# Seven products for two tiles also in the first output projection of a two-layer trunk

## The chip, the cores and the metric

One core of a Trainium2 chip runs the whole program. The metric is the device time of one execution in microseconds. A core has a matrix engine (TensorE, PE in the profile, with its weight loads as PEld), a vector engine (VectorE, DVE), a scalar engine (ScalarE, ACT), GpSimd (POOL) and SyncE (SP), which here only issues transfers. Each engine works through its own list of instructions in order; semaphores tie the lists together.

## The reference

The program computes one inference step of a trunk of two layers for 640 tokens (512 latent tokens and 128 context tokens), with 2048 features in float32:

```python
# for each layer l: 0 is "even", 1 is "odd"
shift, scale, gate = split(silu(cond) @ ada_w[l] + ada_b[l], 3)   # cond: c for latent, c_ctx for context tokens
h = rms_norm(x, norm_g[l]) * (1 + scale) + shift
p = h @ w_in[l]                      # 2048 -> q, k, v, gates, convolution inputs
y = mixers(p)                        # 2048 features: two mixers of 1024 each, each with a SiLU gate
x = x + gate * (y @ w_out[l])        # the output projection, 2048 -> 2048
```

The even layer's mixers are a banded attention and a short gated convolution; the odd layer's are a differential attention and a dense attention. Results are x after the second layer and the new keys and values of the context tokens. The projections have to be of float32 quality.

## The kernel before

*How a product is made.* Activations lie with the features on the 128 partitions: 16 tiles of 128 x 640, called k-tiles. A weight tile is 128 output columns, 16 k-tiles of 128 x 128. TensorE works in a shortened float32 format, so `split` (L242) writes each operand as a high part (ACT, L243) and a low part (DVE, L244), and `proj_q` (L268) adds three products: high x high, high x low, low x high. The tokens go in two halves of 320. A weight tile thus takes 16 x 3 x 2 = 96 matmuls of 128 x 128 by 320 columns.

*Single tiles.* `run_tiles` (L308) takes a list of weight tiles. The first three form a lead phase: for each quarter of four k-tiles the `make_h` function makes the activations (`y0_maker`, L1035, reads y back from DRAM and splits it), and the three tiles use them at once. Then come the other tiles, quarter by quarter; weights are loaded by SP some quarters ahead. After each quarter, `slot` (L300) lets waiting pieces of other work go on: the follow-up of a finished tile (`prep`), the attention (`attn`), and the "fill", a generator that does conditioning work with a rate per slot.

*Pairs.* `run_pairs` (L427) takes two weight tiles together as a 2 x 2 block product of Strassen's kind (Winograd's form): the 2048 features are cut in two halves of eight k-tiles, the tokens in two halves of 320, and seven products of 8 x 3 = 24 matmuls give what two single tiles make of 8. The products are Q1, Q2, N5, P6, P7, Q3, P4. On the weight side, sums of tiles are made on DVE (`operand`, L451, into the tiles sx and sf); on the activation side, four combinations of y (called forms T1 to T4) are made once, by `forms` (L1275). The products are put together by DVE in four pieces of scratch room, which are the memory of the rope tables (`tables`), no longer needed then. Only layer 1's output projection uses this: four single tiles, then six pairs (L1352 to L1395). It brings y in through buffers that are partly those of the odd layer's attention.

*Layer 0's output projection.* All 16 tiles are single (the call at L1102). `out_job` (L1059) adds gate times product to x0, which SP brings back from DRAM, keeps x1 in SBUF in 16 tiles of its own, has POOL save it to DRAM, and adds its squares into `acc` for the next norm. The last tile goes by token halves (`out_last`, L1074): while the second half multiplies, the norm factor of the first half is made. `h1_maker` (L1107) makes the normed input of layer 1 from the x1 tiles.

*Conditioning.* The 6144 columns of `ada_w` per layer go in blocks of 512. Some are made on TensorE at the start; sixteen are made on DVE beside other work: `ada_on_dve` (L171) loads 128 x 512 pieces and adds them up with two accumulations each (L184), 16 pieces a block, and then sums over partitions on TensorE (L190, L196). Nine blocks lie in input projection 0, four in output projection 0, and three, by halves of 256 columns, in input projection 1 (`ada_halves_on_dve`, L204).

*Order.* What follows what on an engine is written by the program in part, and in part set by the scheduler of the framework, which orders instructions by their dependencies. Memory comes from pools ("even", "mid", "odd", "fin"); a pool that opens over one that closed waits for the last users of the memory it lies on. The stretches are: input projection 0 to about 901 us, output projection 0 to 1148, input projection 1 to 2121, output projection 1 to 2347.

Of the kernel before, what the change touches and what calls it, by code (L numbers as in the profile page):

```python
# [11 lines left out]
F32 = mybir.dt.float32  # L12
# [34 lines left out]
N_FILL0 = 9  # L47
N_FILL1 = 13
FILL0 = 0.85
FILL1 = 1.2  # L50
FILL2 = 0.6
# [3 lines left out]
def trunk_kernel(ctx: ExitStack, tc: tile.TileContext, I: dict, O: dict):  # L55
# [115 lines left out]
    def ada_on_dve(blocks, tags=("acc0", "acc1", "adaw", "adaw", "adaw", "ada_sb2")):  # L171
        wt = tags[2:5]
        bufs = 3 if wt[0] == wt[1] else 1
        for l, cb in blocks:
            ap = pools["cur"]
            acc = [ap.tile([P, 512], F32, tag=tags[c], name=f"acc{c}", bufs=1) for c in range(2)]
            for kt in range(KT):
                w = ap.tile([P, 512], F32, tag=wt[kt % 3], name="adaw", bufs=bufs)
                nc.sync.dma_start(w, ada_src(l, cb, kt, 1).rearrange("p k n -> p (k n)"))
                for c in range(2):  # L180
                    if kt == 0:
                        V.tensor_scalar(acc[c], w, sT[:, kt, c:c + 1], None, ALU.mult)
                    else:
                        V.scalar_tensor_tensor(out=acc[c], in0=w, scalar=sT[:, kt, c:c + 1], in1=acc[c],  # L184
                                               op0=ALU.mult, op1=ALU.add)
                yield
# [5 lines left out]
            sb = ap.tile([P, 256], F32, tag=tags[5], name="ada_sb2", bufs=1)  # L192
# [10 lines left out]

    def ada_halves_on_dve(blocks):  # L204

        for l, cb in blocks:
            for h in range(2):
                ap = pools["cur"]
                acc = [ap.tile([P, 256], F32, tag=f"hacc{c}", name=f"hacc{c}", bufs=1) for c in range(2)]
                for kt in range(KT):  # L210
                    w = ap.tile([P, 256], F32, tag="hadaw", name="hadaw", bufs=3)
                    nc.sync.dma_start(w, I["ada_w"][l, kt * P:(kt + 1) * P, cb * 512 + h * 256:cb * 512 + (h + 1) * 256])
                    for c in range(2):
                        if kt == 0:
                            V.tensor_scalar(acc[c], w, sT[:, kt, c:c + 1], None, ALU.mult)
                        else:
                            V.scalar_tensor_tensor(out=acc[c], in0=w, scalar=sT[:, kt, c:c + 1], in1=acc[c],  # L217
                                                   op0=ALU.mult, op1=ALU.add)
                    yield
                s = psT()  # L220
                for c in range(2):
                    PE.matmul(s[32 * c:32 * c + 32, 0:256], ones, acc[c], start=True, stop=True,
                              tile_position=(0, 32 * c))
                sb = ap.tile([64, 256], F32, tag="hsb", name="hsb", bufs=1)
                A.copy(sb, s[0:64, 0:256])
                t = psT()
                for j in range(2):
                    PE.transpose(t[:, j * 64:(j + 1) * 64], sb[:, j * P:(j + 1) * P], ident[0:64, 0:64])
                add_bias(l, cb, t[:, 0:128].rearrange("p (j c x) -> p j c x", j=2, c=2)[:, :, :, 0], h, 2)
                ada_done(l, cb, h, 2)  # L230
                if h == 1:
                    ready.add((l, cb))
                yield
# [74 lines left out]
    def run_tiles(jobs, w_ap, make_h, fill=None, rate=0.0, ahead=None, order=(0, 1, 2, 3), before=None,  # L308
                  last=None, by_half=False, trans=[], grace=0, cut=None, summed=None, led=None):
# [84 lines left out]
        for i in range(lead, len(jobs)):  # L394
# [3 lines left out]
            for qd in range(4):  # L398
                proj_q(pp, parts[t], qd, qd, HV[:1] if split_last else HV)
                if before and qd == 0:  # L400
                    before(i)
                t += 1
                run_ahead(t)
                if pending and not prep:
                    n = pending.pop(0)
                    begin(jobs[n][1], pps[n])
                slot(fill, rate)
# [19 lines left out]
    def run_pairs(cols, w_ap, mov, room, begin, done, more):  # L427
# [46 lines left out]
        MOV = {"Q1": "B11", "Q2": "B21", "N5": "T1", "P6": "T2", "P7": "T3", "Q3": "B22", "P4": "T4"}  # L474
# [11 lines left out]
        def after(p, name, ps):  # L486
# [8 lines left out]
            elif name == "P6":  # L495
                V.tensor_sub(u2, ps, q1)
                V.tensor_sub(u4, st8["n5"], u2)
            elif name == "P7":
# [3 lines left out]
                more(p, u2)  # L502
            elif name == "Q3":
                V.tensor_add(u4, ps, u4)
                done(p, 0, 1, u4)
            else:
                done(p, 1, 0, ps)
# [4 lines left out]
        for i, (p, name) in enumerate(seq):  # L512
            ps, rows_ = pproj.tile([P, 512], F32, tag=f"p{'ab'[i % 2]}{i // 2 % 2}", name="pq")[:, 0:HALF], mov[MOV[name]]
            for h in range(2):
# [6 lines left out]
                if h == 0:  # L521
                    ahead(2 * i + 1)
            after(p, name, ps)
# [3 lines left out]
            elif name in ("P6", "P7"):  # L527
                load(p + 1, "A12" if name == "P6" else "A21")
                if name == "P7":
                    load(p + 1, "A22")  # L530
# [272 lines left out]
    fill1 = ada_on_dve(ada_rest[N_FILL0:N_FILL1])  # L803
    fill2 = ada_halves_on_dve(ada_rest[N_FILL1:])
# [227 lines left out]
    x1 = [None] * KT  # L1032
    make_y0 = y_maker(("q0h", "q0l", "q1h", "q1l"), NT)

    def y0_maker(k):  # L1035
        make_y0(k)
        if k == KT - 1:
            close("even")
            open_pool("mid")
            st["acc"] = pools["cur"].tile([P, NT], F32, name="acc")  # L1040

    def out_load(n):
        st["o", n] = pools["cur"].tile([P, NT], F32, tag="o", name="o", bufs=3)
        nc.sync.dma_start(st["o", n], x0dram[n // 4][:, n % 4 * NT:(n % 4 + 1) * NT])

    def out_before(n):
        if n == 0:
            out_load(0)
        if n + 1 < KT:
            out_load(n + 1)  # L1050

    def out_sum(n, pp, cs):
        if x1[n] is None:
            x1[n] = pools["cur"].tile([P, NT], F32, name=f"x1_{n}")
        for i, dsl, ssl, c in cs:
            V.scalar_tensor_tensor(out=x1[n][:, dsl], in0=pp[i][:, ssl], scalar=hgt[0][:, n, c:c + 1],
                                   in1=st["o", n][:, dsl], op0=ALU.mult, op1=ALU.add)

    def out_job(n):  # L1059
        def f(pp):  # L1060
            mp, acc = pools["cur"], st["acc"]
            need(0, n, fill0)
            out_sum(n, pp, CS)
            nc.gpsimd.dma_start(xdram[n], x1[n])
            if n == 0:
                A.activation(acc, x1[n], AF.Square)
            else:
                sq = mp.tile([P, NT], F32, tag="sq", name="sq", bufs=1)
                A.activation(sq, x1[n], AF.Square)
                V.tensor_add(acc, acc, sq)  # L1070
        return f


    def out_last(pp, h):  # L1074
        n, mp, sl = KT - 1, pools["cur"], HV[h][1]
        out_sum(n, pp, CS[:1] if h == 0 else CS[1:])
        if h == 0:
            st["sq"] = mp.tile([P, NT], F32, tag="sq", name="sq", bufs=1)
            st["rbc"] = mp.tile([P, NT], F32, name="rbc")
        A.activation(st["sq"][:, sl], x1[n][:, sl], AF.Square)  # L1080
# [15 lines left out]
        for b, (o, w) in enumerate(((0, P), (P, P), (2 * P, HALF - 2 * P))):  # L1096
            PE.matmul(rt[:, o:o + w], r[:, b:b + 1].to_broadcast([P, P]), ident[:, P - w:P], start=True, stop=True)
# [350 lines left out]
```

## Time and profile before

| | before |
|---|---|
| time, median of 3 runs | 2356.91 us (2353.24 to 2358.68) |
| profiled execution, time | 2356.86 us |
| profiled execution, span | 2354.9 us |
| TensorE busy | 2309.2 us (98%) |
| VectorE busy | 1477.3 us (63%) |
| ScalarE busy | 905.9 us (38%) |
| mean granted clock of TensorE | 0.995 |

The profile is that of one execution. Its page gives busy time of each engine, the span in slices, the transfers, the chain of work that ended last, and the costliest groups of instructions. In a group's line stand: line of the program and engine, operation, what is written from what (names without buffer numbers), the shape, how many; then busy time and mean ns of one; then the idle time of the engine just before them and what ended it. A row of the timeline gives start, duration, engine, line and operation, and in brackets the idle time before and what ended it. A row of the waits gives which instruction waited for which, the total, how often, and the longest. A row of the transfers gives how many, KB each and the median time from issue to landing. DMA "GB/s" is what all transfers of the core moved.

### The profile page before, as it was taken

The page shows a single profiled execution, that of the slowest core. Times are in us where ns is not written, and L with a number is a line of the kernel's source. Part 1 is how long each engine was busy: PE and PEld are TensorE (multiplying, and loading weights), DVE is VectorE, ACT ScalarE, POOL GpSimd, SP SyncE. Part 2 cuts the span into 40 slices and gives each one's busy share as a digit, 9 for nine tenths or more (in the row PEclk, how much of TensorE's full clock was granted, in tenths as well). Part 3 has the DMA queues.
Part 4 walks back from the last instruction along what each step waited for, and adds up shares of the span by engine and source line. Part 5 has one row for each costly group of instructions (what it writes and reads, how often), then busy time and mean ns, then how long its engine had stood idle before and what let it go on. Part 6 is the DMA issues. An engine that isn't in the chain of part 4 may idle for free.

```text
span 2354.9 us, 41103 instructions
## 1 busy us (share of the span) xinstructions
PE 2309.2 (98%) x16050; PEld 2229.7 (95%) x16050; DVE 1477.3 (63%) x2982; ACT 905.9 (38%) x1898; POOL 130.3 (6%) x175
## 2 busy tenths in 40 slices
PE   6999999999999999999999999999999999999998
PEld 3798999999999999999989999999999999999998
DVE  4459766756845565667874646556464754568775
ACT  4335432433422223222553443434434444445343
POOL 0001000000000000000010100001000001000001
PEclk9999999999999999999999999999999999999999
DMA  9984425425444445666442322313232212128542
GB/s 324 338 265 130 140 70 160 137 66 153 140 131 126 143 137 187 195 188 197 129 126 61 114 73 64 114 56 113 72 99 65 90 49 81 46 73 286 155 135 60
DMA packets 379729, 311.31 MB, mean 132 GB/s; under 512 B 17569, under 2 KB 323294, under 8 KB 379022
## 3 DMA queue, kind: packets, MB, share of 16 engines
q1 hardware_dynamic: 371968, 280.34, 39.4%
q0 software_dynamic: 7024, 28.12, 3.3%
q8 instruction: 126, 2.06, 0.4%
q14 instruction: 69, 0.57, 0.1%
q10 hardware_dynamic: 542, 0.22, 0.0%
HBM read 280.17 MB, written 28.44 MB: 131 GB/s over the span
## 4 chain that ended last, share of the span: by engine, by line
PE 79%; issue 12%; DVE 3%; DMA 2%; ACT 1%; POOL 1%; SPq 1%; ACTq 0%; POOLq 0%; DVEq 0%
PE pa L275 11%; PE pb L276 11%; PE pb L275 11%; PE pb L277 11%; PE pa L276 11%; PE pa L277 11%; PE T L692 2%; PE S L706 1%; PE S L705 1%; PE S L704 1%; PE T L158 1%; DMA ada<-in_ada_w 1%; PE T L753 1%; PE T L755 1%; PE T L754 1%
## 5 line engine op out<-in xcount | busy, mean ns | idle before, releaser
L243 ACT ACTIVATE wh<-raw 128x512 fp32r<-128x512 f32 (+1 forms) x514 | 321.1, 625 | 903.9 <-PE pb L276 762.9
L244 DVE TENSOR_TENSOR wl<-raw,wh 128x512 fp32r<-128x512 f32 (+1 forms) x514 | 350.8, 683 | 454.6 <-ACT wh L243 420.8
L275 PE MATMUL pa<-h,wh 128*128 128x320 f32 x1920 | 610.4, 318 | 1.5 <-ACT h L894 1.2
L276 PE MATMUL pa<-h,wh 128*128 128x320 f32 x1920 | 597.9, 312 | 0.6 <-DVE h L244 0.6
L277 PE MATMUL pa<-h,wl 128*128 128x320 f32 x1920 | 596.1, 310 | 0.0
L275 PE MATMUL pb<-h,wh 128*128 128x320 f32 x1920 | 595.1, 310 | 0.0
L277 PE MATMUL pb<-h,wl 128*128 128x320 f32 x1920 | 594.5, 310 | 0.0
L276 PE MATMUL pb<-h,wh 128*128 128x320 f32 x1920 | 594.3, 310 | 0.0
L275 PEld LDWEIGHTS pa<-h,wh 128*128 128x128 f32 x1920 | 361.9, 189 | 22.0 <-issue 16.9
L276 PEld LDWEIGHTS pa<-h,wh 128*128 128x128 f32 x1920 | 362.9, 189 | 5.0 <-issue 3.3
L277 PEld LDWEIGHTS pa<-h,wl 128*128 128x128 f32 x1920 | 362.3, 189 | 1.3 <-issue 1.2
L277 PEld LDWEIGHTS pb<-h,wl 128*128 128x128 f32 x1920 | 360.8, 188 | 2.5 <-issue 2.5
L276 PEld LDWEIGHTS pb<-h,wh 128*128 128x128 f32 x1920 | 360.9, 188 | 0.8 <-issue 0.8
L275 PEld LDWEIGHTS pb<-h,wh 128*128 128x128 f32 x1920 | 360.9, 188 | 0.6 <-ACT h L894 0.4
L184 DVE SCALAR_TENSOR_TENSOR acc<-adaw,sT,acc 128x512 f32<-128x512 f32 x390 | 275.5, 745 | 10.2 <-DMA adaw<-in_ada_w 9.8
L678 ACT ACTIVATE p<-S,nm,rq 128x768 f32<-128x768 f32 (+3 forms) x120 | 101.2, 844 | 112.9 <-DVE nm L673 84.6
L671 DVE TENSOR_REDUCE nm<-S 128x1 f32<-128x768 f32 (+3 forms) x120 | 91.9, 766 | 18.4 <-PE S L706 17.8
L243 ACT ACTIVATE pth<-T 128x512 fp32r<-128x512 f32 (+1 forms) x132 | 66.0, 533 | 68.1 <-PE T L692 65.9
L244 DVE TENSOR_TENSOR ptl<-T,pth 128x512 fp32r<-128x512 f32 (+1 forms) x132 | 77.7, 608 | 4.8 <-ACT pth L243 3.8
L217 DVE SCALAR_TENSOR_TENSOR hacc<-hadaw,sT,hacc 128x256 f32<-128x256 f32 x180 | 78.0, 478 | 3.1 <-DMA hadaw<-in_ada_w 2.9
L692 PE MATMUL T<-ident,p 128*128 128x128 f32 x452 | 65.1, 273 | 0.1
L520 PE MATMUL pq<-h,wl 128*128 128x320 f32 x192 | 60.1, 313 | 2.9 <-DVE wl L244 2.9
(300 smaller groups left out, 3015.9 us busy)
## 6 DMA issues: line engine op xcount, KB each, us to landing
adaw<-in_ada_w SPq DMA_DIRECT2D x208, 256.0 KB, 2.9
raw<-in_od_w_in SPq DMA_DIRECT2D x208, 256.0 KB, 2.8
raw<-in_ev_w_in SPq DMA_DIRECT2D x202, 256.0 KB, 2.9
ada<-in_ada_w SPq DMA_DIRECT2D x16, 2048.0 KB, 9.9
raw<-in_ev_w_out SPq DMA_DIRECT2D x64, 256.0 KB, 3.7
hadaw<-in_ada_w SPq DMA_DIRECT2D x96, 128.0 KB, 2.2
yd<-y POOLq DMA_DIRECT2D x34, 320.0 KB, 2.9
yin<-yd SPq DMA_DIRECT2D x32, 320.0 KB, 4.1
```

The source lines that it names most:

```text
L158: PE.matmul(acc[32 * g:32 * g + 32, 0:wd], sT[:, kt, :], w[:, kt % m, :], start=(kt < 4), stop=(kt >= KT - 4), tile_position=(0, 32 * g))
L184: V.scalar_tensor_tensor(out=acc[c], in0=w, scalar=sT[:, kt, c:c + 1], in1=acc[c], op0=ALU.mult, op1=ALU.add)
L217: V.scalar_tensor_tensor(out=acc[c], in0=w, scalar=sT[:, kt, c:c + 1], in1=acc[c], op0=ALU.mult, op1=ALU.add)
L243: A.activation(hi, x, AF.Copy)
L244: V.tensor_sub(lo, x, hi)
L275: PE.matmul(ps, wh[:, i, :], hi[:, sl], start=(j == js[0] if alone else (pos == 0 and j == 0)), stop=False)
L276: PE.matmul(ps, wh[:, i, :], lo[:, sl], start=False, stop=False)
L277: PE.matmul(ps, wl[:, i, :], hi[:, sl], start=False, stop=(j == js[1] - 1 if alone else (pos == 3 and j == 3)))
L520: PE.matmul(ps, wl[:, j, :], hi, start=False, stop=(h == 1 and j == 3))
L671: V.tensor_reduce(nm, s, axis=AX.X, op=ALU.max, negate=True)
L678: A.activation(p[:, 0:n], s, AF.Exp, scale=rsc, bias=nm, accum_out=l)
L692: PE.transpose(t[:, i * P:(i + 1) * P], p, ident)
```

## The change

`run_pairs`'s users become one function, `project_out(l, ...)`, that serves both layers, and layer 0's output projection now also goes as four single tiles and six pairs. What comes with it:

- The forms for layer 0 are made while its first tiles run. y comes through three `xr` buffers of 320 KB each, opened in the pool "mid" when the first y tile is made (before: four buffers of the even pool, and "mid" was opened after the last y tile). It is read twice, for the activations and for the forms.
- The x1 tiles are not kept: each is made in an `xr` buffer, saved to DRAM, its squares added, and given up. Six are read back during the last pair (`x1_tail`), eight at the first h of layer 1; the last two stay in their buffers. The rope tables, whose memory is scratch room now in layer 0 as well, are loaded again.
- The last two products of a pair change places (P4, then Q3), and `slot` is called after each half product as well. In the last pair the norm factors (`norm_half`) are made after P4 and after Q3.
- `h1_maker` writes the high part straight from ACT with the bias, and the low part with one DVE operation of the same input.
- The conditioning blocks: 12 in input projection 0 (before 9) at a rate of 1.2 (before 0.85); none in output projection 0; 4 in input projection 1 in parts of 256 columns, but with both parts in one accumulator and one pass over TensorE (before 3, by halves with two passes), at a rate of 0.9 (before 0.6) from the 25th quarter on.
- At the very end the rows of the last tile go out during Q3 and the last to go is the last but one.

```diff
-N_FILL0 = 9
-N_FILL1 = 13
-FILL0 = 0.85
-FILL1 = 1.2
-FILL2 = 0.6
+N_FILL0 = 12
+FILL0 = 1.2
+FILL1 = 0.9
+FILL1_FROM = 24
...
-        MOV = {"Q1": "B11", "Q2": "B21", "N5": "T1", "P6": "T2", "P7": "T3", "Q3": "B22", "P4": "T4"}
+        MOV = {"Q1": "B11", "Q2": "B21", "N5": "T1", "P6": "T2", "P7": "T3", "P4": "T4", "Q3": "B22"}
...
                 if h == 0:
                     ahead(2 * i + 1)
+                    slot()
             after(p, name, ps)
...
+    def late_yin(k):
+        t = pools["cur"].tile([P, NT], F32, tag="xr", name="yin", bufs=3)
+        nc.sync.dma_start(t, ydram[k])
+        split(*new_h(k), t)
...
     def y0_maker(k):
-        make_y0(k)
-        if k == KT - 1:
+        if k == 0:
             close("even")
             open_pool("mid")
             st["acc"] = pools["cur"].tile([P, NT], F32, name="acc")
+            st["sq"] = pools["cur"].tile([P, NT], F32, name="sq")
+            attn.append(forms())
+        late_yin(k)
...
+    def x1_done(n):
+        nc.gpsimd.dma_start(xdram[n], st["xr", n])
+        squares(n)
+
+    def x1_last(t, h):
+        n, sl = KT - 2 + t, HV[h][1]
+        if t == h:
+            squares(n, sl)
+            return
+        nc.gpsimd.dma_start(xdram[n], st["xr", n])
+        prep.append(norm_half(n, h))
+        if h:
+            drain(prep)
...
+    def x1_tail(name):
+
+        for k in (range(0, 4) if name == "P6" else range(4, 6)):
+            x1_back(k, big("w8", bufs=4) if k < 4 else big("sx" if k == 4 else "sf"))
+
+    def x1_back(k, t, i=0):
+        x1[k] = t[:, i * NT:(i + 1) * NT]
+        nc.sync.dma_start(x1[k], xdram[k])
+
+    project_out(0, y0_maker, x1_done, x1_last, x1_tail)
...
     def h1_maker(k, hv):
+        if k == 0 and hv[0][0] == 0:
+            for g in range(3):
+                t = big(f"T{g}")
+                for i in range(3 if g < 2 else 2):
+                    x1_back(6 + 3 * g + i, t, i)
+            for i in (14, 15):
+                x1[i] = st["xr", i]
+            nc.sync.dma_start(tables, I["k_tables"])
...
-            A.activation(t[:, sl], t[:, sl], AF.Identity, bias=mod[1][:, k, c:c + 1])
-        al = slice(hv[0][1].start, hv[-1][1].stop)
-        split(hi[:, al], lo[:, al], t[:, al])
+            A.activation(hi[:, sl], t[:, sl], AF.Identity, bias=mod[1][:, k, c:c + 1])
+        for sl, c in toks:
+            V.scalar_tensor_tensor(out=lo[:, sl], in0=t[:, sl], scalar=mod[1][:, k, c:c + 1], in1=hi[:, sl],
+                                   op0=ALU.add, op1=ALU.subtract)
```

The function that both layers now call:

```python
    def project_out(l, maker, finish, last, tail):
        w = W_OUT[l]
...
        go_on = run_tiles([(n * P, job(n)) for n in range(N_SINGLE - 1)], w, maker, order=(0, 2, 1, 3))
        n = N_SINGLE - 1
        parts = [split_w(load_raw(w, n * P, qd)) for qd in range(4)]
        go_on()
        pp = new_pp(0)
        for hv in (HV[1:], HV[:1]):
            for qd in range(4):
                proj_q(pp, parts[qd], qd, qd, hv)
                advance(attn, 2)
                go_on()
            if hv == HV[1:]:
                drain(attn)
                for j in range(8):
                    hi, lo = hs[j]
                    split(hi[:, HALF:NT], lo[:, HALF:NT], t1[j])
...
        run_pairs([(n * P, (n + 1) * P) for n in range(N_SINGLE, KT, 2)], w,
                  {"B11": half_of(0, 0), "T1": half_of(0, 1), "B21": half_of(8, 0), "B22": half_of(8, 1),
                   "T2": form_of(0), "T3": form_of(1), "T4": form_of(2)}, room, begin, part, done, tail)
        drain(prep)
```

361 lines of the change are left out of this document (161 added, 200 removed).

## The prediction

> **What bounds the kernel now.** I read the page's first part and the chain of waits, then the durations of the matmuls one by one, then busy time by stretch.
>
> ```profile
> span 2354.9 us, 41103 instructions
> PE 2309.2 (98%) x16050; PEld 2229.7 (95%) x16050; DVE 1477.3 (63%) x2982; ACT 905.9 (38%) x1898; POOL 130.3 (6%) x175
> PE 79%; issue 12%; DVE 3%; DMA 2%; ACT 1%; POOL 1%; SPq 1%; ACTq 0%; POOLq 0%; DVEq 0%
> ```
>
> TensorE is busy nearly all the time and carries the chain, so time goes with the matmuls and with TensorE's gaps. What one matmul costs is read from the timeline by their starts, since neighbours overlap:
>
> ```profile
> 1146.22 0.31 PE L275 MATMUL pb<-h,wh 128*128 128x320 f32 x1
> ...
> 1147.83 0.31 PE L277 MATMUL pb<-h,wl 128*128 128x320 f32 x1
> ```
>
> Each lasts 0.31, but eleven steps lie between these two starts: 1.61/11 = 146.4 ns each. Where DVE could come to bound is seen in busy time by stretch (columns: span, then busy time and instructions of PE, PEld, DVE, ACT, POOL, then granted clock, DMA share, GB/s):
>
> ```profile
> 160.00:400.00 240.00, 236.49 (x1680) 229.32 (x1679) 177.44 (x374) 99.27 (x226) 13.65 (x14) 1.00 0.47 142
> 400.00:600.00 200.00, 199.87 (x1416) 194.61 (x1415) 125.39 (x251) 79.35 (x176) 9.71 (x10) 1.00 0.38 112
> 2121.00:2187.00 66.00, 63.52 (x434) 62.56 (x434) 55.24 (x98) 34.65 (x58) 5.48 (x9) 1.00 0.93 296
> 2187.00:2200.00 13.00, 9.79 (x56) 9.25 (x55) 6.22 (x9) 2.86 (x6) 0.41 (x1) 0.87 0.38 101
> 2200.00:2340.00 140.00, 140.00 (x970) 139.91 (x969) 105.30 (x174) 57.25 (x103) 13.77 (x22) 1.00 0.40 113
> ```
>
> The last three rows are layer 1's output projection, which already works with four single tiles and six pairs. They are the nearest picture of what layer 0 becomes: the lead phase (all of y loaded, split and combined into forms) loses 2.5 us of TensorE, the start of the pairs loses about 3 in a gap, and the steady pairs lose nothing with DVE 75% busy. The waits of TensorE name the same places:
>
> ```profile
> PE T L543 <- DVE m L588: 5.5, 4, 3.1
> PE pq L520 <- DVE wl L244: 2.9, 1, 2.9
> PE T L543 <- ACT ot L1318: 2.3, 1, 2.3
> ```
>
> **The change part by part.**
>
> *Matmuls.* A tile takes 16 k-tiles x 3 products x 2 halves = 96 matmuls; a pair takes 7 x 24 = 168 where two tiles take 192. Six pairs save 6 x 24 = 144 matmuls: 144 x 146.4 ns = **-21.1 us**, all on the path. Both ends are the same here.
>
> *Conditioning passes on TensorE.* Each block ends with sums over partitions on TensorE:
>
> ```profile
> 901.05 0.31 PE L277 MATMUL pb<-h,wl 128*128 128x320 f32 x1
> 901.29 0.64 PE L190 MATMUL T<-acc,ones 128*32 128x256 f32 x8
> 901.86 0.41 PE L275 MATMUL pa<-h,wh 128*128 128x320 f32 x1
> ```
>
> From the matmul before to the one after are 0.81 us, 0.66 over the usual step, and two transposes follow: about 0.8 a pass, an estimate. Before there are 13 whole blocks and 3 in two halves, 19 passes; after, 16. Three passes fewer: **-2.4** (-3 to 0).
>
> *The boundary from input to output projection 0.* The rows above also show that there is no gap now: the first four y tiles were brought in earlier, into buffers that the old maker names. After, the maker closes the memory of the input projection when it makes its first tile, and loads y through three buffers that lie in that memory. Reading after's order of instructions: the first load on SP waits for the last gate multiplication of y, which waits for the last matmul of the input projection, and TensorE has no matmul in between that doesn't need this y. The chain of that tile, all of it now bare:
>
> ```profile
> 901.25 0.63 ACT L243 ACTIVATE wh<-raw 128x512 fp32r<-128x512 f32 x1 [2.89 <-PE pb L276]
> L967 ACT ACTIVATE gt_t<-pb 128x320 f32<-128x320 f32 x1 | 0.4, 418 | 0.0
> L968 DVE SCALAR_TENSOR_TENSOR gg<-gt_t,pb 128x320 f32<-128x320 f32 x1 | 0.5, 480 | 0.0
> L970 DVE TENSOR_TENSOR y<-y,gg 128x640 f32<-128x640 f32 x1 | 0.8, 818 | 0.0
> yin<-yd SPq DMA_DIRECT2D x32, 320.0 KB, 4.1
> adaw<-in_ada_w SPq DMA_DIRECT2D x208, 256.0 KB, 2.9
> L243 ACT ACTIVATE h<-yin 128x640 fp32r<-128x640 f32 x16 | 11.5, 732 | 12.0 <-DMA yin<-yd 8.2 <-PE pb L277 2.2 <-PE pb L276 1.5
> L244 DVE TENSOR_TENSOR h<-yin,h 128x640 fp32r<-128x640 f32 x16 | 13.0, 822 | 9.1 <-ACT h L243 9.0
> ```
>
> ACT splits a weight first (0.63), then tanh 0.42, DVE 0.48 and 0.82, the load 4.1, ACT 0.73: 7.2 us from the last matmul to the first. The first weights are ahead of it on SP; the next two y loads queue behind it and land together. After a gap the clock is slow for a while, as layer 1's start of the pairs shows:
>
> ```profile
> 2187.81 0.31 PE L519 MATMUL pq<-h,wh 128*128 128x320 f32 x1
> 2191.02 0.42 PE L520 MATMUL pq<-h,wl 128*128 128x320 f32 x1 [2.90 <-DVE wl L244]
> 2193.37 0.47 PE L518 MATMUL pq<-h,wh 128*128 128x320 f32 x1
> 2193.64 0.47 PE L519 MATMUL pq<-h,wh 128*128 128x320 f32 x1
> ```
>
> The step there is 0.27 instead of 0.146. The row of 2187 to 2200 has a mean clock of 0.87, so 13 x 0.13/0.5 = 3.4 us at half clock, which cost 3.4 x (1 - 0.146/0.27) = 1.5. With 0.7 for the second and third y tile, which need their DVE half (0.82) too: **+9.4**. Low end 6 (load at 2.9 and no slow stretch); high end 14 (an estimate: the load at 6.5 because the forms' loads share the engines, and a slow stretch of twice the length).
>
> *Lead phase.* Loads of y twice (2 x 16 x 320 KB) and four tiles of weights, eight sets of forms on DVE. Layer 1 does the same work and loses 2.5 us in the row of 2121 to 2187, most of it in one wait of 2.3 on an output copy that layer 0 doesn't have; but layer 1 has four further buffers for y and here there are three, and a y load that waits for one holds back the weight loads behind it on SP. I take **+2** (0 to 10; the high end is priced as a rival).
>
> *Start of the pairs.* Layer 1's stall (2.9 and the slow stretch, 5 in all) came from weight buffers that the forms held. In layer 0 the order of instructions puts the forms' end and the weight loads of the first pair well before the fourth tile ends, so I take **0** (0 to +5). Layer 1 keeps its own.
>
> *Steady pairs.* DVE gets saves to DRAM and squares with an addition per tile: 2 x 0.82 more in a pair's 168 x 0.146 = 24.6 us, on 105.3/140 = 75%: 82%. Nothing waits for it; **0** (0 to +3). POOL issues the saves; it is 6% busy.
>
> *Boundary to input projection 1.* Now:
>
> ```profile
> 1141.24 0.80 PE L1088 MATMUL T<-ones,sq 128*128 128x1 f32 x6 [0.46 <-DVE ss L1090]
> ...
> 1149.66 0.41 PE L276 MATMUL pa<-h,wh 128*128 128x320 f32 x1 [0.41 <-DVE h L244]
> 1152.07 1.54 PE L1097 MATMUL T<-ident,r 128*128 128x128 f32 x6 [0.70 <-POOL r L1093]
> 1155.52 0.47 PE L275 MATMUL pa<-h,wh 128*128 128x320 f32 x1
> ...
> 1158.61 0.33 PE L277 MATMUL pa<-h,wl 128*128 128x320 f32 x1
> ```
>
> Between 1147.83 and 1158.61 some 10.8 us pass for 24 matmuls of 146 ns (3.5): 7.3 lost, part of it to the norm of the last half, part to the slow clock. The norm of half 0 inside the last tile adds, with 0.8 for such a group of small matmuls and three groups, about 2: 9.3. After, the norm of half 0 runs under the last product (3.5 us of matmuls) and half 1's before the first matmul of layer 1: a chain as long as today's from 1147.83 to the first full-speed step, about 10 us from the last-but-one product to the first h, less 3.5 hidden, and 1.5 to 2 of slow clock: 8.3. **-1** (-3 to +5). The first x1 tiles are back by then; eight more (320 KB each) and the tables, 768 KB, are issued on SP after the last-but-one product and must land behind the first input matmuls.
>
> *Fills.* Input projection 0 takes three blocks more, 3 x 16 x 2 accumulations at 745 ns (the row of the accumulation):
>
> ```profile
> L184 DVE SCALAR_TENSOR_TENSOR acc<-adaw,sT,acc 128x512 f32<-128x512 f32 x390 | 275.5, 745 | 10.2 <-DMA adaw<-in_ada_w 9.8
> L217 DVE SCALAR_TENSOR_TENSOR hacc<-hadaw,sT,hacc 128x256 f32<-128x256 f32 x180 | 78.0, 478 | 3.1 <-DMA hadaw<-in_ada_w 2.9
> ```
>
> That is 96 x 0.745 = 71.5 us of DVE. The rate goes from 0.85 to 1.2 blocks' steps a slot, so the end of the filling stays about where it is; up to 600 us DVE goes from (177.4 + 125.4)/440 = 69% to some 84%, and in the first stretch from 74% to near 90%. In that stretch TensorE lost 240 - 236.5 = 3.5 us with 74%. **+3** (0 to +15). Input projection 1 gets 64 more steps of 256 wide, 64 x 0.478 = 31 us on a DVE that has room (its busiest waits, 5.5 us on the row of m, stay): **0** (-2 to +3).
>
> *Tail.*
>
> ```profile
> 2348.20 1.06 PE L543 MATMUL T<-ident,xr 128*128 128x128 f32 x5
> 2350.97 0.54 POOL L1321 DMA_DIRECT2D out_y_prompt<-ot  x1
> ```
>
> The last tile but one went out by POOL last, at 2351. After, one of the two last tiles goes out during the last product and the end hangs on the other half tile's short path through SP and ACT: **-1.2** (-2.5 to 0).
>
> Sum: -21.1 - 2.4 + 9.4 + 2 - 1 + 3 - 1.2 = -11.3. The profiled run took 2356.86 us (2.0 outside the span), the median of the runs is 2356.91, so both bases agree: **2345.5 us**.
>
> One rule of the Trainium skill comes out otherwise at the boundary to layer 1. "TensorE: Matmul & The Clock Gate", section "What's actually happening", says that the slow clock follows a whole idle window of about 3.4 us. By it the short waits there (0.4, 0.7 and the like) would cost no slow stretch after the change, and the sum would be 2343.5; this case's trace shows 0.27 steps at 1155.5 without one idle stretch of that length, so I keep the measured price.
>
> **The rivals.**
>
> *A. The first boundary is cheap.* The load of y may start before the gate is done if its buffer falls on memory freed earlier. Then 9.4 becomes about 1 and the rest stays: 2337. For it: today there is no gap at that place. Against: the first load's wait stands in after's instructions.
>
> *B. DVE becomes the bound in input projection 0, and it ends slower.* DVE works in order, so an accumulation ahead of a softmax step delays TensorE. At 74% the stretch to 400 us lost 3.5 us; at 90% a queue of 1.49-us pairs stands ahead of every urgent step. If four tenths of the 71.5 us come through as waits, +28.6 replaces +3: 2371. From a fifth (14.3) on, the gain is nil; for it speaks the wait of 3.1 on DVE's m, against it that 400 to 600 us lost 0.13 with 63%.
>
> *C. Loads bind the lead phase.* Three buffers, each held for a load and its two splits: at 4.1 + 0.73 + 0.82 = 5.65 us, 16 loads take 16 x 5.65/3 = 30 us, inside the 42 us that three tiles (288 matmuls) take; with loads at 6.5 under a DMA share of 0.93 they take 43 us and bind. Then lead +8 instead of +2, start of the pairs +4: 2355.5, no change.
>
> *D. x1 or the tables come back late.* Eight tiles and the tables, 3.3 MB at the 296 GB/s of the lead row: 11 us, beside weights; half of that bare gives about +5: 2350.5. For it: all of them are issued at the same moment as the first weights. Against: an h tile is wanted only every few us.
>
> *E. The saving doesn't appear.* If half products left gaps, the 144 would buy nothing; layer 1's 970 instructions in 140.00 busy us exclude that.
>
> **How the numbers follow.** My forecast's case (2337 to 2352, D included) gets 0.50, A 0.13, C 0.19, B 0.18. A measurement of this kernel tells 0.2% (4.7 us) from no change, so faster means below 2352.2: the forecast's case (0.50), A (0.13) and a little of C (0.04): 0.67. Same: most of C and a little of B: 0.15. Slower: most of B and C's worst: 0.18. The range goes from 2334 (A with a cheap boundary to layer 1) to 2364 (B half way); the likeliest case's own is 2337 to 2352.
>
> **What would show it.** Right: 144 fewer matmuls at 146 ns; one gap of about 7 us before the first matmul of the output projection, ended by ACT's h after a DMA yin, with steps of 0.27 behind it; steady pairs with TensorE 100% busy; TensorE waits in 160 to 600 us up by a few us only. Wrong: no gap there (A); PE waits on DVE in input projection 0 over 14 us (B); repeated waits for yin, or a gap at the first product of a pair in layer 0 (C); waits on x1 or tables after 1140 us (D).

## The result and the profile after

The changed kernel takes 2345.45 us (median of 5 runs, 2341.5 to 2347.92) where the kernel before takes 2354.12 us (median of 5, 2353.11 to 2358.68): a ratio of 0.9955, with a 95% interval of 0.994 to 0.9971. The profiled execution took 2347.92 us with a span of 2345.9, against 2356.86 and 2354.9 before: -9.0 us of span. The medians lie 8.7 us apart; the ratio stands for 10.6 us (6.8 to 14.1). The prediction said 2345.5 us, and -11.3 us on the profiled execution of before.

The first lines of the page of the changed kernel and its chain that ended last:

```profile
span 2345.9 us, 41233 instructions
PE 2286.9 (97%) x15900; PEld 2207.9 (94%) x15900; DVE 1577.8 (67%) x3187; ACT 932.9 (40%) x1934; POOL 129.7 (6%) x175
PE 87%; DMA 5%; DVE 4%; issue 2%; ACT 2%; SPq 1%; POOL 0%; ACTq 0%; DVEq 0%; POOLq 0%
```

TensorE is busy for 22 us less (2286.9 against 2309.2), but the span is only 9 us shorter: TensorE stands idle for 13 us more. A slow step counts as busy in this view. The waits of TensorE in the changed kernel name the largest one, which stands in no row of before:

```profile
PE pa L247 <- ACT h L215: 7.9, 2, 7.5
PE T L523 <- DVE m L568: 6.0, 4, 3.2
...
PE pa L248 <- DVE h L216: 2.8, 4, 1.1
```

Where it lies is seen best by stage. The projections' matmuls have a fixed number in each stage, so the start of the first and of the last of them marks the stage in every trace (in us; the columns add up to the span):

| stage | before | after | change |
|---|---|---|---|
| to the first projection matmul | 48.78 | 49.80 | +1.0 |
| input projection 0 | 867.34 | 871.19 | +3.9 |
| its last to output projection 0's first matmul | 0.15 | 7.77 | +7.6 |
| output projection 0, first 384 matmuls (four tiles) | 56.32 | 62.04 | +5.7 |
| output projection 0, the rest | 175.25 | 149.20 | -26.1 |
| boundary and the first 300 matmuls of input projection 1 | 51.94 | 51.28 | -0.7 |
| input projection 1, the rest | 926.87 | 927.55 | +0.7 |
| output projection 1 | 220.22 | 222.02 | +1.8 |
| last matmul's start to the end | 7.99 | 5.01 | -3.0 |

Each column is one execution, and single executions vary: three traces of the changed kernel have 870.5 to 871.7 in the second row, 61.7 to 66.4 in the fourth and 49.8 to 52.4 in the sixth. A change of 1 or 2 us in one row says little.

The timeline of TensorE in the changed kernel at the third row of the table:

```profile
920.99 0.31 PE L249 MATMUL pb<-h,wl 128*128 128x320 f32 x1
928.76 0.63 PE L247 MATMUL pa<-h,wh 128*128 128x320 f32 x1 [7.46 <-ACT h L215]
...
931.67 0.47 PE L249 MATMUL pa<-h,wl 128*128 128x320 f32 x1
931.94 0.47 PE L247 MATMUL pa<-h,wh 128*128 128x320 f32 x1
...
933.50 0.31 PE L248 MATMUL pb<-h,wh 128*128 128x320 f32 x1
933.64 0.31 PE L249 MATMUL pb<-h,wl 128*128 128x320 f32 x1
```

and the other engines in that gap:

```profile
921.19 0.63 ACT L215 ACTIVATE wh<-raw 128x512 fp32r<-128x512 f32 x1 [1.18 <-PE pb L248]
921.72 0.42 ACT L946 ACTIVATE gt_t<-pb 128x320 f32<-128x320 f32 x1
...
922.46 0.48 DVE L947 SCALAR_TENSOR_TENSOR gg<-gt_t,pb 128x320 f32<-128x320 f32 x1
922.97 0.82 DVE L949 TENSOR_TENSOR y<-y,gg 128x640 f32<-128x640 f32 x1
923.87 1.29 SPq L1064 DMA_DIRECT2D yin<-yd  x3
```

It is the chain that was forecast: tanh, the two DVE steps of the last gate, and only then the first load of y, which is split on ACT at 927.97. Behind the gap the steps are 0.27 us until 933.3, then 0.146. The granted clock goes with it (columns: window, its length, busy time and instructions of PE, PEld, DVE, ACT, POOL, granted clock, DMA share, GB/s):

```profile
920.00:926.60 6.60, 1.30 (x9) 1.03 (x8) 2.40 (x4) 0.96 (x3) 0.54 (x1) 1.00 0.51 134
926.60:933.40 6.80, 4.42 (x14) 3.72 (x15) 3.79 (x7) 2.80 (x4) 0.00 (x0) 0.50 0.99 371
```

It falls to half within the gap, at 926.6, and comes back at 933.4.

The windows of the changed kernel show the two stages that the forecast kept at nothing or nearly so (columns as above):

```profile
160.00:400.00 240.00, 236.11 (x1682) 228.61 (x1680) 194.54 (x407) 99.02 (x226) 13.33 (x15) 1.00 0.52 157
990.00:1139.00 149.00, 149.00 (x1020) 148.80 (x1019) 122.35 (x205) 63.69 (x104) 6.47 (x12) 1.00 0.47 140
```

With DVE at 81% instead of 74% in the first, TensorE is as busy as before (236.11 of 240 against 236.49). In the second, the steady pairs of layer 0, it is busy all the time with DVE at 82%.

At the boundary to layer 1 the steps are slow again, and at the end POOL is done with its last output while the matmuls still run:

```profile
1140.15 0.83 PE L1186 MATMUL T<-ident,r 128*128 128x128 f32 x6
1140.81 0.78 PE L1177 MATMUL T<-ones,acc 128*128 128x1 f32 x6
1141.94 0.80 PE L1177 MATMUL T<-ones,sq 128*128 128x1 f32 x6 [0.34 <-ACT sq L1169]
1144.18 0.88 PE L1186 MATMUL T<-ident,r 128*128 128x128 f32 x6 [1.45 <-POOL r L1182]
1144.88 0.73 PE L247 MATMUL pa<-h,wh 128*128 128x320 f32 x2
...
1145.67 0.47 PE L248 MATMUL pa<-h,wh 128*128 128x320 f32 x1
1145.93 0.47 PE L249 MATMUL pa<-h,wl 128*128 128x320 f32 x1
```

```profile
2340.70 0.76 POOL L1383 DMA_DIRECT2D out_y_sample<-ot  x1 [21.45 <-ACT ot L1382]
2340.84 0.31 PE L496 MATMUL pq<-h,wl 128*128 128x320 f32 x1
2341.45 0.54 POOL L1384 DMA_DIRECT2D out_y_prompt<-ot  x1
2342.71 0.39 SPq L1403 DMA_DIRECT2D out_y_sample<-ot  x1
2343.04 0.38 ACTq L1407 DMA_DIRECT2D out_y_prompt<-ot  x1
```

### The profile page after: what moved, and what is told of

Read it like the earlier page. It is cut to its first block, busy times and chain, and to the rows that moved or that the text cites. A ratio compares the mean times of both kernels' runs of the same rounds, so it can differ in the third digit from the quotient of the medians.

```text
span 2345.9 us, 41233 instructions
## 1 busy us (share of the span) xinstructions
PE 2286.9 (97%) x15900; PEld 2207.9 (94%) x15900; DVE 1577.8 (67%) x3187; ACT 932.9 (40%) x1934; POOL 129.7 (6%) x175
## 4 chain that ended last, share of the span: by engine, by line
PE 87%; DMA 5%; DVE 4%; issue 2%; ACT 2%; SPq 1%; POOL 0%; ACTq 0%; DVEq 0%; POOLq 0%
PE pa L247 10%; PE pb L247 10%; PE pb L248 10%; PE pb L249 10%; PE pa L248 10%; PE pa L249 10%; PE pq L494 4%; PE pq L496 4%; PE pq L495 4%; PE T L672 2%; DMA yin<-yd 2%; PE S L684 1%; PE S L686 1%; PE S L685 1%; DMA ada<-in_ada_w 1%
## 5 line engine op out<-in xcount | busy, mean ns | idle before, releaser
L247 PE MATMUL pa<-h,wh 128*128 128x320 f32 x1728 | 552.0, 320 | 10.6 <-ACT h L215 7.9
L248 PE MATMUL pa<-h,wh 128*128 128x320 f32 x1728 | 538.5, 312 | 2.8 <-DVE h L216 2.8
L249 PE MATMUL pa<-h,wl 128*128 128x320 f32 x1728 | 536.3, 310 | 0.0
L247 PE MATMUL pb<-h,wh 128*128 128x320 f32 x1728 | 535.8, 310 | 0.0
L249 PE MATMUL pb<-h,wl 128*128 128x320 f32 x1728 | 535.7, 310 | 0.0
L248 PE MATMUL pb<-h,wh 128*128 128x320 f32 x1728 | 535.1, 310 | 0.0
L187 DVE SCALAR_TENSOR_TENSOR acc<-adaw,sT,acc 128x512 f32<-128x512 f32 (+1 forms) x600 | 358.2, 640 | 16.3 <-DMA adaw<-in_ada_w 15.6
L247 PEld LDWEIGHTS pa<-h,wh 128*128 128x128 f32 x1728 | 326.5, 189 | 30.1 <-issue 14.9
L248 PEld LDWEIGHTS pa<-h,wh 128*128 128x128 f32 x1728 | 327.2, 189 | 8.5 <-issue 4.2
L247 PEld LDWEIGHTS pb<-h,wh 128*128 128x128 f32 x1728 | 325.3, 188 | 0.9 <-issue 0.4
L248 PEld LDWEIGHTS pb<-h,wh 128*128 128x128 f32 x1728 | 325.1, 188 | 0.1
L496 PE MATMUL pq<-h,wl 128*128 128x320 f32 x384 | 119.2, 311 | 3.1 <-DVE wl L216 3.1
L494 PE MATMUL pq<-h,wh 128*128 128x320 f32 x384 | 120.5, 314 | 0.3 <-DVE xr L1059 0.3
L495 PE MATMUL pq<-h,wh 128*128 128x320 f32 x384 | 119.1, 310 | 0.0
L495 PE MATMUL pq<-T,wh 128*128 128x320 f32 x288 | 88.8, 308 | 0.0
## 6 DMA issues: line engine op xcount, KB each, us to landing
ada<-in_ada_w SPq DMA_DIRECT2D x16, 2048.0 KB, 10.1
```

Source lines behind the costliest of these rows:

```text
L187: V.scalar_tensor_tensor(out=a, in0=w, scalar=sT[:, kt, c:c + 1], in1=a, op0=ALU.mult, op1=ALU.add)
L247: PE.matmul(ps, wh[:, i, :], hi[:, sl], start=(j == js[0] if alone else (pos == 0 and j == 0)), stop=False)
L248: PE.matmul(ps, wh[:, i, :], lo[:, sl], start=False, stop=False)
L249: PE.matmul(ps, wl[:, i, :], hi[:, sl], start=False, stop=(j == js[1] - 1 if alone else (pos == 3 and j == 3)))
L494: PE.matmul(ps, wh[:, j, :], hi, start=(h == 0 and j == 0), stop=False)
L495: PE.matmul(ps, wh[:, j, :], lo, start=False, stop=False)
```

## The experiments

My theory: the pairs give what their count of matmuls says, the late y loads at the first boundary take most of it back, and DVE is nowhere the bound. The rivals to be told apart: the DMA's share or DVE makes the loss wherever y is loaded; the fuller DVE in input projection 0 costs more than it seems; the moved conditioning blocks and not the pairs make the gain.

The stages of all traces (us, as in the table above; "boundary 1" is the third row, "four tiles" the fourth, "rest of out 0" the fifth):

| | after, again | early_y | fill16 | before_fill | both | warm | both_wide | after, third |
|---|---|---|---|---|---|---|---|---|
| to the first projection matmul | 49.28 | 49.12 | 50.20 | 51.17 | 49.27 | 50.79 | 48.83 | 50.66 |
| input projection 0 | 871.66 | 869.01 | 877.30 | 871.52 | 875.64 | 868.87 | 876.92 | 870.52 |
| boundary 1 | 7.19 | 0.15 | 7.52 | 0.15 | 0.15 | 9.01 | 0.15 | 6.96 |
| four tiles | 66.39 | 61.11 | 63.14 | 56.32 | 63.00 | 62.07 | 63.30 | 61.70 |
| rest of out 0 | 149.20 | 149.60 | 149.20 | 170.91 | 150.68 | 149.20 | 151.83 | 149.20 |
| boundary 2 and 300 matmuls | 49.83 | 52.51 | 52.26 | 48.24 | 51.22 | 52.61 | 51.32 | 52.35 |
| rest of input projection 1 | 926.73 | 928.06 | 914.72 | 933.12 | 914.67 | 923.35 | 914.70 | 926.91 |
| output projection 1 | 221.89 | 222.33 | 222.18 | 220.77 | 219.77 | 223.79 | 221.13 | 222.98 |
| to the end | 5.01 | 5.02 | 4.99 | 7.98 | 4.98 | 5.02 | 5.47 | 5.02 |

**The changed kernel again**, beside the next three on the same chip.

> The changed kernel once more, for comparison on the same chip: 8 to 10 us under the kernel before, with the gap of 7.5 us before the first matmul of output projection 0.

2347.6 us against 2354.51 for the kernel before: 0.9968 (0.9956 to 0.9979), some 7 us by the medians and so a little less than expected, and the gap is there (7.2 us from start to start). The four tiles take 66.39 here, 62.04 in the first profile and 61.70 in a third. What makes this trace longer is a second fall of the clock in the lead phase, at a wait for a y tile:

```profile
959.21 0.64 PE L247 MATMUL pa<-h,wh 128*128 128x320 f32 x1 [2.07 <-ACT h L215]
```

In the window from just before that row the granted clock is 0.50:

```profile
958.60:965.40 6.80, 6.19 (x23) 6.19 (x24) 5.02 (x8) 3.39 (x5) 0.00 (x0) 0.50 0.85 269
```

The 23 steps from 959.21 on take 2.9 us more than at 0.1464.

**Early y tiles.** The first four y tiles go through the buffers that before used, and the memory is opened one quarter later:

```diff
+    make_y0 = y_maker(("q0h", "q0l", "q1h", "q1l"), NT)
+
     def y0_maker(k):
-        if k == 0:
+        if k < 4:
+            make_y0(k)
+            return
+        if k == 8:
             close("even")
```

> The changed kernel, but its first four y tiles come through the q0/q1 buffers of the input projection, as before the change, and the memory of the output projection is opened at the second quarter of k-tiles. My theory: the gap of 7.5 us before the first matmul of the output projection and the slow clock behind it (about 3 us) are the price of the late buffers and of nothing else; the gap goes, the time falls by 8 to 11 us against the changed kernel, to about 2336, and what the lead phase loses later (2.7 us in waits for y) stays or grows by at most 3. Rival: loads and DVE bind the lead phase, and the gap only moves to the second quarter, where the y tiles now queue with the forms: the time falls by less than 4 us.

2338.87 us, 8.7 us less than the changed kernel on the same chip (ratio to before 0.9927, 0.9914 to 0.9939). The timeline of TensorE in early_y at that place:

```profile
918.13 0.31 PE L249 MATMUL pb<-h,wl 128*128 128x320 f32 x1
918.28 0.31 PE L247 MATMUL pa<-h,wh 128*128 128x320 f32 x1
...
945.68 0.41 PE L247 MATMUL pa<-h,wh 128*128 128x320 f32 x1 [1.75 <-ACT h L215]
```

The gap is gone, and the slow steps behind it; the granted clock is 1.00 from 918 to 980 us. So the late buffers made them. (The edit also lets the forms begin a quarter later.) But the four tiles still take 61.11 us where 384 matmuls at 0.1464 need 56.2; the changed kernel's three traces have 61.70 to 66.39, of which the slow steps make 2.5 to 6.2. What the lead phase loses beside the slow steps stays, with waits for the y tiles of later quarters, as at 945.68. The rival has that much right.

**All conditioning blocks in input projection 0.**

```diff
-N_FILL0 = 12
-FILL0 = 1.2
+N_FILL0 = 16
+FILL0 = 1.6
```

> The changed kernel with all sixteen conditioning blocks in input projection 0 (rate 1.6 instead of 1.2), none later. My theory: DVE is not the bound there; four more blocks cost input projection 0 four passes over TensorE (3.2 us) and 1 to 3 us of waits, and give the passes back in input projection 1, so -1 to +3 us against the changed kernel. Rival: at over 90% busy DVE delays the attention, a fifth or more of the added 95 us of DVE work comes through as waits of TensorE: +15 us or more.

2342.86 us, 4.7 us less than the changed kernel: better than my theory allowed (-1 to +3), and the rival's +15 is far off, though DVE stays a little under the 90% that it speaks of. In fill16 the window to 400 us reads:

```profile
160.00:400.00 240.00, 236.15 (x1672) 226.16 (x1671) 210.94 (x436) 99.93 (x227) 13.94 (x15) 1.00 0.58 172
```

DVE is 88% busy there, and TensorE no less busy than with 74% in before. Input projection 0 gets 5.6 us longer (877.30 against 871.66), of which four passes at about 0.8 are 3.2. The gain is in input projection 1, which is 12.0 us shorter without its four blocks (926.73 to 914.72). Passes explain 3.2 of them. The waits of TensorE for 1190 to 2110 us, first in the changed kernel and then in fill16, show another part:

```profile
PE T L523 <- DVE m L568: 4.9, 3, 3.2
PE S L684 <- ACT p L658: 1.5, 2, 1.0
PE T L523 <- DVE k1l L216: 1.0, 2, 0.8
```

```profile
PE T L523 <- DVE m L568: 0.8, 2, 0.4
PE T L523 <- DVE k0l L216: 0.8, 1, 0.8
```

The wait of 3.2 us on DVE's m, which before has too, comes with the conditioning steps in input projection 1. The clock pays too: in the changed kernel it is at 0.50 from 1203.1 to 1209.9, behind that wait, and in fill16 it is 1.00 from 1157 to 2114. So a block there cost 3.0 us, and one in input projection 0 about 1.4; both and early_y below, which differ by the same blocks, give 3.3 and 1.7. The two prices are not for quite the same work: a block is 32 accumulations of 512 columns (22 us of DVE) in input projection 0 and 64 of 256 columns (27 us) in input projection 1. How much of the difference belongs to the stage and how much to the form wasn't tried.

**The conditioning blocks moved, without the pairs.** The kernel before with

```diff
-N_FILL0 = 9
-N_FILL1 = 13
-FILL0 = 0.85
+N_FILL0 = 12
+N_FILL1 = 12
+FILL0 = 1.2
 FILL1 = 1.2
-FILL2 = 0.6
+FILL2 = 0.8
```

> The kernel before with only the conditioning blocks moved: 12 in input projection 0 at a rate of 1.2, none in output projection 0, 4 by halves in input projection 1 at a rate of 0.8. My theory: moving blocks changes little; input projection 0 gets 2.4 us of passes and 1.5 us of waits, output projection 0 loses 3.2 us, two more half passes cost 1.6 us, and the boundary to input projection 1 gains 1: about +1 us (-2 to +4) against the kernel before, so that the gain of the change is that of the pairs. Rival: the blocks in output projection 0 were a cause of its losses at the boundary, and moving them alone gives 4 us or more.

2359.42 us, a ratio of 1.0016 (1.0006 to 1.0026): slower than the kernel before by 4.9 us of the medians, 0.9 beyond my range, or by 3.8 us as the ratio has it, just inside. Moving the blocks is no cause of the gain. With none of them in output projection 0 on either side, its rest takes 170.91 us with single tiles and 149.20 with pairs: -21.7 us, where 144 matmuls at 146.4 ns are 21.1. Input projection 1 pays here: behind the boundary 933.12 against 926.87 in before, with a fourth block in halves. The boundary and its 300 matmuls give 3.7 back (48.24 against 51.94): before has a conditioning pass there, at 1153.5, and a granted clock of 0.50 from 1151.8 to 1158.6; before_fill has no pass there and a clock of 1.00 from 1150 to 1200. The rival is right about that place, and wrong about the time of the kernel. Of the 4.9 us, 2.4 lie ahead of the first projection matmul in the profiled execution (51.17 against 48.78), where nothing was changed.

**The gap filled.** The changed kernel with work on TensorE in the gap:

```diff
         if k == 0:
+            t = psT()
+            for i in range(32):
+                PE.transpose(t[:, i % 4 * P:(i % 4 + 1) * P], y[KT - 1][:, i % 5 * P:(i % 5 + 1) * P], ident)
             close("even")
```

> The changed kernel with 32 extra transposes of the last y tile on TensorE, put ahead of the output projection: they start when the last gate multiplication ends (about 2.9 us into the gap), their result is not used, and they are done before the first load of y is split. They fill the gap with work, so only the slow clock behind it is disputed. My theory: the slow steps of 0.27 behind the gap are the clock's answer to the idle stretch, and with the gap filled the first matmuls step at 0.147: 1.5 to 3 us less than the changed kernel. Rival: the clock is slow there whatever fills the gap, or the matmuls are held by the y tiles anyway: within 1 us of the changed kernel.

2345.89 us, against 2345.45 of the changed kernel on the same chip: no difference. The timeline of warm:

```profile
919.66 0.31 PE L249 MATMUL pb<-h,wl 128*128 128x320 f32 x1
922.52 3.71 PE L1140 MATMUL T<-ident,y 128*128 128x128 f32 x32 [2.56 <-DVE y L949]
928.66 0.63 PE L247 MATMUL pa<-h,wh 128*128 128x320 f32 x1 [2.43 <-ACT h L215]
...
931.57 0.47 PE L247 MATMUL pa<-h,wh 128*128 128x320 f32 x1
931.84 0.47 PE L248 MATMUL pb<-h,wh 128*128 128x320 f32 x1
```

The steps behind it are still 0.27. The transposes cut the idle time into two rests of 2.56 and 2.43 us, and the granted clock reads:

```profile
920.00:928.50 8.50, 3.71 (x32) 3.48 (x32) 1.91 (x3) 1.44 (x3) 0.54 (x1) 1.00 0.68 226
928.50:935.30 6.80, 6.45 (x22) 5.97 (x23) 6.07 (x10) 3.33 (x5) 0.00 (x0) 0.50 0.71 242
```

The clock is still at 1.00 over the transposes and both rests, and falls to 0.50 as the first matmuls start, for 6.8 us. That is 8.9 us behind the start of the last matmul of the input projection; in the three traces of the changed kernel it falls 2.5 to 5.6 us behind it, within the gap, and stays down for 6.8 to 10.2. So in this one trace the fall came later and still came, and all of the slow stretch lies on matmuls. The boundary is longer too (9.01 us): the first load of y takes 5.3 us from its issue to its split, against 4.1 in the changed kernel. My expectation failed; whether a gap filled without a rest would do it wasn't tried.

**Early y tiles and all blocks in input projection 0.** Both edits together.

> Early y tiles (as in early_y) and all sixteen conditioning blocks in input projection 0 (as in fill16). If the two gains have separate causes they add: about 8.7 + 4.7 = 13 us less than the changed kernel, 2334. Rival: with DVE fuller in input projection 0, the early y loads and splits are late and the gap comes back in part: 8 us less or smaller.

2332.49 us, a ratio of 0.99 (0.9884 to 0.9915) to before, and 13.0 us under the changed kernel on the same chip (2345.45): the two gains add, as expected. The start of the pairs in layer 0 now shows a wait, which the changed kernel doesn't have:

```profile
988.05 0.42 PE L494 MATMUL pq<-h,wh 128*128 128x320 f32 x1 [1.95 <-ACT wh L215]
```

This is the fastest version here.

**More buffers for y.** As both, with the second quarter's y tiles in the memory of the forms T7 to T4:

```diff
             attn.append(forms())
-        late_yin(k)
+        if 8 <= k < 12:
+            t = big(f"T{15 - k}")[:, 0:NT]
+            nc.sync.dma_start(t, ydram[k])
+            split(*new_h(k), t)
+        else:
+            late_yin(k)
```

> As both, and the y tiles of the second quarter too come through buffers of their own (memory of four forms that are made later), so that the three shared buffers carry only the third and fourth quarter. My theory: the waits left in the lead phase of early_y (1.9 and 0.8 us, for y tiles) come from the three shared buffers, and 1 to 3 us of them go. Rival: they come from the DMA's share (16 y tiles read twice beside weights) and nothing changes, within 1 us of both.

2339.47 us, 7.0 us more than both. The four tiles take 63.30 us against 63.00. That row ends where the first matmul of the pairs starts, and so holds the wait there, which is longer than in both:

```profile
989.19 0.60 PE L494 MATMUL pq<-h,wh 128*128 128x320 f32 x1 [2.97 <-DVE xr L1059]
```

Without what this one step costs over 0.146 (3.1 us here, 2.1 in both) the four tiles take 60.2 and 60.9: the lead phase itself gains 0.7 us at most, less than the 1 to 3 of my theory and no more than executions vary by. So the three shared buffers are not shown to be what it waits for. What is left of its loss (some 4 to 5 us over 56.2) stays open between the DMA's share and the order on ACT and DVE. Of the 7.0 us, the profiles (spans of 2333.6 and 2329.4) show 4.2, among them 1.5 in output projection 0 (63.30 + 151.83 against 63.00 + 150.68), where the clock is at 0.50 behind the wait for 6.8 us and in both for 3.4, and 3.1 behind the first four tiles of output projection 1 (160.38 against 157.29), which this edit doesn't touch: there TensorE waits 3.4 us for DVE's wl in both_wide and 1.6 in both, and only in both_wide does the clock fall. How much of the rest is the edit's isn't settled.

**The changed kernel a third time**, beside the last three.

> The changed kernel again, for comparison on the same chip: 7 to 9 us under the kernel before.

2345.45 us against 2355.68: 0.9958 (0.9942 to 0.9974). That is 10.2 us by the medians, above the 7 to 9 expected; the three comparisons give 6.9 to 10.2 us.

## Why the prediction was right, and where not

*Matmuls, -21.1.* Right: -21.7 between before_fill and the changed kernel. Neither has conditioning blocks in that stage; they differ there by the pairs and by what comes with them, the saves and squares of x1 and the order of the norm.

*Passes, -2.4.* Output projection 0 fell by 4.3 us when its four blocks left (175.25 to 170.91 in before_fill), a little over one us each and more than the 0.8 a pass; the three that were added in input projection 0 come with +3.2 to +4.3 in all, over four traces.

*First boundary, +9.4.* The gap was forecast at 7.2 and is 7.5 (6.6 to 7.5 in three traces), step by step as the chain said, and rival A is excluded. One reading was wrong on the way: the rows at 901 us show no boundary of the projections, and input projection 0 doesn't end there. That tile is the last but one; the last matmul of input projection 0 and the first of output projection 0 in before are these:

```profile
916.12 0.31 PE L277 MATMUL pb<-h,wl 128*128 128x320 f32 x1
916.26 0.31 PE L275 MATMUL pa<-h,wh 128*128 128x320 f32 x1
```

There is no gap at that place either, so the sum wasn't harmed. The slow steps were sized at 1.5, which is too small; from 928.76 to 933.50 there are 14 steps in 4.74 us, 2.7 us more than 14 x 0.1464, of which one wait of 0.22 is for y. Counted so, without the wait, the slow steps behind the gap cost 2.5, 3.2 and 2.9 us in the three traces. The second and third y tile were given 0.7 and took that 0.22. In all some 10 us stand against 9.4.

*Lead phase, +2.* Somewhat too small. The +5.7 of the table's row holds the slow steps of the boundary; without slow steps the four tiles lose 3.3, 3.9 and 2.5 us in the three traces of the changed kernel, and 4.8 in early_y. That the size is near owes something to luck. The row of layer 1, at 2121 to 2187, was read as losing 2.5 us of TensorE; by starts of matmuls its four tiles take 61.02 us, 4.8 over 56.2. About 2.4 of these belong to the wait on the output copy, and about 1.5 to 15 transposes (L543), which count as busy; layer 0 has neither there, and little of that row speaks for the waits for y that layer 0 has. Rival C named the place. Its price of 8 for the lead was not reached by loads: the +10.1 of the second trace is slow clock for 6.2.

*Start of the pairs and steady pairs, 0.* Right for the changed kernel: 149.00 of 149.00 us busy. A wait at the start appears in both and both_wide.

*Second boundary, -1.* Near: -0.7 in the table, -2.1 and +0.4 in the other two traces, and no wait for x1 or the tables stands in the changed kernel's rows there (rival D). The number hides two parts that weren't forecast: in before_fill (one trace), moving the blocks alone gives -3.7 at this place, and the changed kernel's three traces are 1.6 to 4.1 slower there than that. The weighing of the clock's rule came out as the row had it in two traces of three: the page of the Trainium skill, "TensorE: Matmul & The Clock Gate" ("What's actually happening"), asks for a whole idle window of about 3.4 us before the clock drops. At 1145 the steps are 0.27 where the longest wait in the rows shown is 1.45 us. By the rule as I read it there would have been none. In the second trace there are none.

*Fills, +3.* Input projection 0 got 3.9 us longer, 2.4 of it passes: 1.5 of waits, half of the forecast and far from rival B's price. Its condition didn't arise: DVE was forecast near 90% in the first stretch and 84% up to 600 us and is at 81% and 78%, since a third of the added accumulations (32 of 96) falls behind 600 us. Fill16 shows how far B's point lies: at 88% DVE there the loss is still small. In input projection 1 I had 0, and two passes fewer (1.6) besides; it is +0.7. By fill16 a block there costs 3.0 us, so the fourth block was not free.

*Tail, -1.2.* Too small, and out of its range: -3.0. The end moved from 8.0 to 5.0 us behind the start of the last matmul. POOL's two issues (0.76 and 0.54) and the copies ahead of them stood behind the last matmul, and are now under the last product.

*Not forecast:* output projection 1 is 1.8 us longer in the changed kernel (222.02 against 220.22; 221.89 and 222.98 in the other two traces). It wasn't followed up; over all ten traces this stage goes from 219.78 to 223.79.

The sum was -11.3, the span shows -9.0, the medians -8.7. With the terms of the sum put into the stages of the table (a pass at 0.8), the forecast of a stage is off by up to 2.3 us, and the misses have both signs: input projection 0 -1.5, the first boundary with the four tiles +1.9, the rest of output projection 0 -1.8, input projection 1 +2.3, output projection 1 +1.8, the end -1.8, the start +1.0. The mechanism held; that the total is so near is in part luck. That 2345.45 meets 2345.5 is luck again, of the base: the median of before was 2356.91 over three runs and is 2354.12 over five, and this fall of 2.8 hides that the gain, by the medians, was smaller than forecast.

## What to carry to other kernels

A cut in the bound engine's work is worth its full count only where the stage stays fed: here 21.7 us were cut and some 13 given back, 9 of them (early_y) at the one place where a buffer came free later than before. So ask of each new buffer which old one it lies on, and follow the order of instructions from that one's last user; that chain could be priced to within 0.6 us from rows of the old trace. Before background work is moved, price a unit of it in each place: a block cost 1.4 to 1.7 us in one stage and 3.0 to 3.3 in another, and the stage with the fuller engine was the cheaper one, though the block's form differed too. And take the slow clock out of a stage's time before reading waits from it: of the 10.1 us that one trace lost in the four tiles, 6.2 were slow steps.

## What was not expected of the hardware

At the boundary to layer 1 three traces of the changed kernel show the same two waits of TensorE, 0.34 and 1.45 us, ahead of the first matmuls, and three different clocks there (the first trace, the second, the third):

```profile
1145.10:1148.40 3.30, 3.30 (x14) 3.30 (x14) 2.52 (x8) 2.28 (x6) 0.00 (x0) 0.50 1.10 357
1143.90:1150.00 6.10, 4.30 (x34) 4.16 (x34) 4.54 (x12) 3.69 (x8) 1.70 (x2) 1.00 1.02 405
1142.20:1148.90 6.70, 5.67 (x22) 5.67 (x23) 5.26 (x15) 3.83 (x10) 0.98 (x1) 0.50 0.95 331
```

So a slow stretch can come where no wait is longer than 1.45 us, and the same waits can come without one. With 3.7 us of transposes in the gap the clock stayed at 1.00 until the matmuls began, and was then at half for 6.8 us; without them it fell within the gap, for 6.8 to 10.2. What decides in these cases stays open; between executions of one kernel it moves the time by some us, as the four tiles show.
